# Expert blocks of 96 + 32 slots issued as four column strips of 32 slots on TensorE

## The chip, the cores and the metric

One core of one Trainium2 chip runs the whole program; nothing is shared with other cores. The metric is the device time of one execution in microseconds (us), as the median of several runs. In the profile PE is TensorE's matmul row, PEld its weight loads, DVE VectorE, ACT ScalarE, POOL GpSimd, SP SyncE.

## What is computed

One layer on 512 latent tokens (and 256 context tokens) of width 1024: an RWKV-7 head group and an HGRN2 head group behind one input projection, an output projection, and then a mixture of experts, where this change lies:

```python
def _swiglu(x, wg, wu, wd):
    return (jax.nn.silu(x @ wg) * (x @ wu)) @ wd

scores = jax.nn.sigmoid(h @ router_w)
...
_, top_e = lax.top_k(sel, TOP_K)              # 8 of 64 experts for each of the 512 tokens
gate = gate / jnp.sum(gate, axis=-1, keepdims=True) * ROUTE_SCALE
...
def step(out, inp):
    tok, gw, e = inp                          # a block of slots of one expert
    y = _swiglu(h[tok], wg[e], wu[e], wd[e]) * gw[:, None]
    return out.at[tok].add(y), None
```

Each expert has three float32 matrices: gate and up of 1024 x 256, down of 256 x 1024, 1 MB each, 3 MB in all. Every expert's weights are read from memory once.

## The kernel before

The first 1090 us of the program (mixers, output projection, router, shared expert) are not touched. What follows is the routed experts, until about 1942 us, and a final norm.

**Blocks.** Experts are ranked by size. A block has 128 slots (tokens) on 128 rows of the result. Of the 46 blocks 25 have one expert on all 128 slots, 11 have two experts with 64 slots each, and 10 (`NMIX`) have a larger expert on slots 0 to 95 and one of the smallest on slots 96 to 127. The last two kinds need the weights of two experts: 6 MB. The three are called whole, 64 + 64 and 96 + 32 here. A list written at line 1650 mixes the kinds in proportion.

**One block.** `front` (line 1726) makes `xT`, the block's tokens transposed: for 30 blocks an indirect DMA on POOL's queue gathers the rows (line 1740) and TensorE transposes them (line 1746); for 16 blocks TensorE picks them from rows on chip with 96 small matmuls (line 1735). `ffn_in` (line 1462) multiplies: for each of 8 tiles of 128 channels, `xT` is the stationary operand and the weights, gate beside up, 512 columns, are the moving one (line 1467). `ffn_out` (line 1470) applies silu on ACT (line 1472) and the product on DVE (`av`, line 1474), transposes on TensorE (line 1478), copies on ACT (`at`, line 1480), and multiplies with the down weights, 2 halves of 512 columns by 2 tiles (line 1485). `add_rows` (line 1681) scales the result on DVE (`rows`, line 1686) and adds it to the sums in memory with an indirect DMA of 512 KB on POOL's queue (line 1687).

A block's experts are given as `halves`, a list of (slots, activations, weights). Each half is one matmul instruction per tile, which writes the rows of its slots in one PSUM bank:

```python
for kt in range(8):
    for r, lhs, w in halves:
        pe.matmul(pg[r], lhs(kt), w[0][:, :, kt * 256:kt * 256 + 256], start=(kt == 0), stop=(kt == 7))
```

A column strip is the part of TensorE's array whose columns write certain rows of the result: a half on slots 64 to 127 occupies the columns 64 to 127. Instructions on different columns can run at the same time.

**Order.** TensorE works in program order: `xT` and line 1467 of a block, then lines 1478 and 1485 of the block before it. A scheduler lays out the instructions of each engine; the small matmuls of line 1735 and the lists (line 1628: which tokens a later block takes) fill places between.

**Weights.** SP's queue issues one DMA of 1 MB each for gate, up and down of one expert after another (`load`, line 1371, the DMA at line 1378). A load waits for two things: that the load two places before it has landed (`LAG` = 2 in flight), and that its buffer is free. There are five buffers for experts (`NWL` + `NWR`), so a load waits for the matmuls of the expert five places before it.

**Lists and sums.** The list of a block (`li`, line 1634, DVE) has four buffers, and the scatter of line 1687 reads it. So the list of block i + 4 waits until the scatter of block i has landed, and DVE, which works in order, has the products `av` and the `rows` of later blocks behind it. The gather and the scatter stand in one queue on POOL.

Of the kernel before, what the change touches and what calls it, by code (L numbers as in the profile page):

```python
# [8 lines left out]
F32 = mybir.dt.float32  # L9
FR = mybir.dt.float32r  # L10
# [13 lines left out]
NWL, NWR = 4, 1               # buffers for the weights of experts  # L24
LAG = 2                      # loads in flight
ONPE = range(12, 44, 2)      # blocks whose rows TensorE picks, from rows on chip; the others' come by DMA
HB = 4                       # block from which on these rows are loaded
NP = 4                       # experts whose weights come before the routing is known: they rank last
# experts by size: NONE have a block of 128 slots each, NMIX 96 slots of a block, NTWO are two to a block, and the
# smallest NMIX have the other 32 slots of the former  # L30
NONE, NMIX = 18, 10
NTWO = 64 - NP - NONE - 2 * NMIX
# pairs in the output projection, in the order in which they are ready
OUT = [[('rw', 0), ('hg', 0)], [('rw', 1), ('rw', 2)], [('hg', 1), ('hg', 2)], [('hg', 3), ('rw', 3)]]
# priorities of the streams along their steps, and the number of steps; smaller ones go first
# [11 lines left out]
def hybrid_layer(ctx, tc, x, c, xctx, c_ctx, w_mod, b_mod, norm1_g, norm2_g, w_in, rw_conv, rw_w0, rw_w2,  # L47
# [29 lines left out]
    # ---------------------------------------------------------------- constants  # L77
# [24 lines left out]
    # masks of the chunk scores, rows (B s | K s) for d 0 and (K s | B s) for d 1, columns (A t | R t)  # L102
# [11 lines left out]
    # scan resets  # L114
# [6 lines left out]
    # masks of the 32-token blocks of HGRN2, for two heads  # L121
# [15 lines left out]
    hTh = hp.tile([128, 8, NT], FR)             # hT = hTh + hTl, each exact in float32r  # L137
# [14 lines left out]
    # conditioning vectors, then per-channel vectors, rows of 128 turned into columns  # L152
# [13 lines left out]
    lo = const.tile([128, 2, 8], F32)          # lb, 1 - lb  # L166
# [9 lines left out]
    def vectors():  # L176
# [20 lines left out]
        # lower bounds of HGRN2: softmax over the two rows, first entry  # L197
        l3 = vc[:, VR['hlb']:VR['hlb'] + 16].rearrange("p (d l j) -> p d l j", d=2, l=2)
        lv = lbt.rearrange("p (d j) k -> p d j k", d=2)
        # softmax with its maximum: k 0 max, 1 e0, 2 e1, 3 sum  # L200
# [10 lines left out]
    # adaLN: silu of the conditioning vectors as a stationary operand  # L211
# [24 lines left out]
    # operands of a step of the scan, both directions: (K' B')^T d, (A | R) d, scores d h, inverses h  # L236
    WCT = {False: 64, True: 128}
    PKW = {lat: 256 + 6 * w + 128 for lat, w in WCT.items()}
    # operands of HGRN2: queries and gates, values with tokens on partitions, forget gates
# [9 lines left out]
    H2_d = dt("h2", (NACC, D))                  # rows that unused slots take are zero  # L249
    ACC = dt("acc", (2 * NACC, D))              # sums of the routed experts, the first and the second of a block  # L250
    X_d = dt("xl", (128, 512))                  # of the blocks beyond the slots: per token, slot and gate
# [3 lines left out]
    # until the scans begin, the place of the mixers' results serves the convolutions  # L255
    cv_a = pers.tile([128, 2048], F32, tag="y_rw")
    cv_b = pers.tile([128, 2048], F32, tag="y_hg")
    PC = const.tile([128, 4, 2, NCH], F32)      # decay of a chunk: pair, direction, step
    # ------------------------------------------------------------------ streams of work
    # The mixers run as streams that take turns, in steps; what a step needs of other streams is in marks.  # L260
# [6 lines left out]
    def banks(names):  # L267
        """PSUM in turns"""
        names = list(names)

        def get(name):
            names.append(names.pop(0))
            return psb(names[-1], name)
        return get

    # ---------------------------------------------------------------- projection
    # tiles of 128 columns: decay, rate, gate of RWKV-7; for pairs of heads its r, k, v or HGRN2's q, g, i, f
    porder = [(0, 'rw'), (1, 'rw'), (0, 'hg'), (2, 'rw'), (1, 'hg'), (3, 'rw'), (2, 'hg'), (3, 'hg')]
    NP1 = 6                  # of these before the scans begin
# [6 lines left out]
    def s_weights():  # L286
        """weights of the tiles, as the sum of two float32r parts"""
# [16 lines left out]
    # ------------------------------------------------- norm 1, adaLN, transposes  # L304
# [81 lines left out]
    def tok_major(src, dst, alloc):  # L386
        """dst [128, 6, 128] <- src [128, NT] transposed, tokens on partitions"""
        for g0, g1 in ((0, 4), (4, 6)):
            pt = alloc("p_tok")
            for g in range(g0, g1):  # L390
                pe.transpose(pt[:, (g - g0) * 128:(g - g0) * 128 + 128], src[:, g * 128:g * 128 + 128], ident)
            yield
            act.activation(dst[:, g0:g1].rearrange("p g v -> p (g v)"), pt[:, 0:(g1 - g0) * 128], AF.Copy)
            yield

    # ------------------------------- RWKV-7: operands of the scan, scores and inverses of the chunks
# [3 lines left out]
    y_0 = cpa.tile([128, SEQ], F32)              # result of the pair of heads that is scanned first  # L400
# [21 lines left out]
    def conv(n, m, pl, pcx, dst, out_):  # L422
        """dst [128, NT] (or lat only) <- depthwise conv of projection tile m"""
# [39 lines left out]
    def turned(src, dst):  # L463
        """tokens on partitions, to memory"""
# [5 lines left out]
    def s_evac():  # L470
        """what becomes of the projection's tiles"""
# [70 lines left out]
    def rw_head(j):  # L542
# [4 lines left out]
        # 1 / norm per head and token, with the tokens on partitions, spread over the channels again  # L547
# [29 lines left out]
    def rw_gates(j, d):  # L577
        """decay and rate of a direction, and what follows from them"""
# [23 lines left out]
        o = 1 - d                      # P_t at columns o .. o+63, 1 at the other end  # L602
        pool.memset(px[:, :, 64 * d:64 * d + 1], 1.0)
        act.activation(px[:, :, o:o + 64], cs.rearrange("p (c t) -> p c t", t=64), AF.Exp, scale=-KAPPA)
        act.activation(cs, cs, AF.Exp, scale=KAPPA)          # 1 / P
# [4 lines left out]
        # of the bonus, r times k over both directions  # L610
# [10 lines left out]
    def rw_oper(j, d):  # L621
        """operands of the scores in a direction"""
# [5 lines left out]
        # chunks in the order of the steps; tokens of A and B reversed within a chunk for d 1  # L628
# [31 lines left out]
    def pk(j, lat, f0, f1, rows=slice(0, 128)):  # L660
        """columns f0 .. f1 of the operands of the steps of pair j, as [rows, steps, columns]"""
# [10 lines left out]
    def rw_scores(j, d):  # L672
        """scores of the chunks in one direction, and the operands of the scan to memory"""
# [3 lines left out]
        for n in range(0, NCH, 2):  # L677
# [4 lines left out]
            st = xq.tile([128, 2, 2, 2, 64], F32, name="SC", bufs=2)             # step, A | R, h, t  # L682
# [19 lines left out]
        # the operands that the scan takes, K and B decayed to the end of the chunk  # L702
# [17 lines left out]
    def rw_bonus(j):  # L720
        """sum over the head of r * (kd_f + kd_b) * r_k, times v"""
# [12 lines left out]
    def s_scores():  # L734
        for j in range(4):
            if j > 1:
                yield from need(('merged', j - 2))
            st_[j]["SA"] = xq.tile([128, NCH, 2, 64], F32, name="SA", bufs=2)     # triangular parts, columns B s, A t
# [6 lines left out]
    def rw_inverse(j):  # L745
        """unit triangular systems: the inverses of the 32 x 32 blocks (d, q, n, h) on the diagonal, one to a partition"""
# [25 lines left out]
        # inverses of the 64 x 64 systems from those of the blocks on the diagonal: B^-1 = D + D U D  # L772
# [44 lines left out]
    def head_norm(sq, bank, eps):  # L817
        """1 / sqrt(mean + eps) per head and token of squares sq, over the head's channels in bank; tokens lie on
        partitions in between"""
# [29 lines left out]
    # ------------------------------------------------------------------- scan of RWKV-7 over the chunks  # L849
# [94 lines left out]
    def rw_out(j, pl, psn):  # L944
        """group norm, bonus, gate"""
# [30 lines left out]
    def inverse_tiles():  # L976
        """likewise, in the place of the inverses'"""
# [24 lines left out]
    def y_of(kind, j):  # L1002
        """result of a pair of heads, and its rows of the output projection"""
        return (y_0 if j == 0 else y_rw[:, j]) if kind == 'rw' else y_hg[:, j], j if kind == 'rw' else 4 + j

    # ------------------------------------------------------------------ HGRN2
    def hgrn_pair(j, hq, psg):
# [8 lines left out]
        for d in range(2):  # L1016
# [41 lines left out]
            # products of the decays of a group's four 32-blocks, in processing order  # L1058
# [14 lines left out]
            # level 1: later 32-block of a 64 against the earlier; level 2: later 64 against the earlier  # L1073
            qe4 = qe.rearrange("p (g n) b -> p g n b", n=4)
            ke4 = ke.rearrange("p (g n) b -> p g n b", n=4)
            qsec, ksec = (2, 0) if d == 0 else (0, 2)      # first block of the later and of the earlier 64
            odd = 1 - d                                    # parity of the later block of a 64
# [11 lines left out]
            # states at the borders of groups  # L1089
# [10 lines left out]
            # scores  # L1100
# [75 lines left out]
    # ------------------------------------ rest of adaLN, and HGRN2's part of the output projection  # L1176
    def s_mod(psm):
        """remaining adaLN rows, without their bias: g1, sh2, sc2, g2"""
# [45 lines left out]
    def out_rows(w, kind, j):  # L1224
        """rows of the output projection"""
# [4 lines left out]
    def s_out(pl, psm):  # L1230
        """the residual with the output projection of pairs as they are ready"""
# [3 lines left out]
        # sums that the routed experts add to, and rows for unused slots  # L1235
# [15 lines left out]
        for group in OUT:  # L1251
            ws = []
            for kind, j in group:
                # the last weights come early, to where the first pairs of HGRN2 were
# [23 lines left out]
    def run(done, waiting=""):  # L1278
        """the streams in turns, until those in done have ended and those in waiting wait for a mark"""
# [61 lines left out]
    # ===================================== output projection, norm 2, router, shared expert  # L1341
    psc[0] = ctx.enter_context(tc.tile_pool(name="psC", bufs=1, space=PSUM, reuse_waits="tile"))
    late = ctx.enter_context(tc.tile_pool(name="late", bufs=1, reuse_waits="tile"))
    # blocks of slots: the first NONE experts, second blocks of the largest five, pairs, 96 and 32 slots, the last NP
# [557 lines left out]
```

## Time and profile before

| | before |
|---|---|
| median of 3 runs | 1969.67 us (1947.13 to 1979.79) |
| span of the profiled execution | 1964.3 us (5.4 us under the median; it has no other time of its own) |
| TensorE busy | 1777.6 us, 90% |
| DVE, ACT, POOL busy | 753.9, 618.5, 395.2 us |
| moved by DMA | 401.65 MB, mean 204 GB/s |
| routed experts, 1095 to 1930 us of the span | 835 us |

A matmul's end in the trace is modelled: instructions follow each other 0.43 us apart where each is shown as 0.592 us long. So the time of a group is read from its first start to its last end in the timeline, and not from the mean of one. A float32 matmul of the program stands as two matmuls and two weight loads in the trace. A busy share is an average over a stretch.

### The profile page before, as it was taken

What the parts mean: (1) busy time and instruction counts of PE and PEld (TensorE: products, weight loads), DVE (VectorE), ACT (ScalarE), POOL (GpSimd) and SP (SyncE); (2) the same over time, 40 slices, a digit from 0 to 9 for tenths busy, and PEclk for the clock granted to TensorE, in tenths of its full rate; (3) what the DMA queues carried; (4) which work ended last, traced back from release to release, by engine and by line L of the source; (5) the groups of instructions that cost most, each with busy time, mean ns of one, the idle gap of its engine ahead of it and who ended that gap; (6) DMA issues with size and microseconds to landing.
All of it is one profiled execution on the core that took longest, in us unless ns stands there. A gap on an engine that the chain in (4) does not pass through costs nothing. (4 is left out here: it accounts for less than half of the span.)

```text
span 1964.3 us, 25497 instructions
## 1 busy us (share of the span) xinstructions
PE 1777.6 (90%) x9675; PEld 1004.8 (51%) x9675; DVE 753.9 (38%) x1722; ACT 618.5 (31%) x1286; POOL 395.2 (20%) x372
## 2 busy tenths in 40 slices
PE   5998989999699999898999889988899999799983
PEld 2766676675577775564455443333344443433431
DVE  4566685847563344433446332111121121111113
ACT  5463535345143353421323232111121221111121
POOL 2233223313221242231230012100111110101111
PEclk9977988998579977687999989999899999899987
DMA  7313555554565354533437877995967999758975
GB/s 257 94 50 108 148 137 147 174 137 134 129 210 144 114 185 139 169 128 124 141 124 281 296 259 245 333 348 204 318 204 249 311 324 335 247 187 296 350 238 161
DMA packets 200252, 401.65 MB, mean 204 GB/s; under 512 B 41804, under 2 KB 132009, under 8 KB 175168
## 3 DMA queue, kind: packets, MB, share of 16 engines
q1 hardware_dynamic: 188768, 360.05, 53.0%
q0 software_dynamic: 11360, 39.96, 9.1%
q8 instruction: 77, 1.26, 0.3%
q14 instruction: 47, 0.39, 0.1%
HBM read 323.66 MB, written 73.15 MB: 202 GB/s over the span
## 5 line engine op out<-in xcount | busy, mean ns | idle before, releaser
L1467 PE MATMUL p_gu<-wgu,xT 128*64 128x512 f32 (+3 forms) x1104 | 424.1, 605 | 0.4 <-ACT xT L1458 0.4
L1467 PEld LDWEIGHTS p_gu<-wgu,xT 128*64 128x64 f32 (+3 forms) x1104 | 129.1, 155 | 254.0 <-issue 240.2
L1485 PE MATMUL p_y<-wd,at 128*64 128x512 f32 (+3 forms) x584 | 240.8, 636 | 4.4 <-ACT at L1480 3.0
L369 PE MATMUL p_proj<-hTh,w_hi 128*128 128x512 f32 (+1 forms) x456 | 181.5, 398 | 6.0 <-ACT w_hi L296 3.1
L370 PE MATMUL p_proj<-hTh,w_lo 128*128 128x512 f32 (+1 forms) x456 | 176.3, 388 | 3.8 <-DVE w_lo L298 3.8
L371 PE MATMUL p_proj<-hTl,w_hi 128*128 128x512 f32 (+1 forms) x456 | 177.3, 390 | 2.3 <-POOL hTl L351 1.7
L1687 POOL DMA_INDIRECT acc<-rows,li x46 | 74.3, 1616 | 463.6 <-DVE rows L1686 443.4
L1634 DVE SCALAR_TENSOR_TENSOR li<-lv,bpr 128x2 int32<-128x2 f32 x46 | 10.1, 219 | 401.1 <-DMA acc<-rows,li 287.9
L1485 PEld LDWEIGHTS p_y<-wd,at 128*64 128x64 f32 (+3 forms) x584 | 71.2, 162 | 141.8 <-issue 124.0
L1472 ACT ACTIVATE sl<-p_gu 128x256 f32<-128x256 f32 x50 | 19.2, 384 | 384.9 <-PE p_gu L1467 383.4
L1458 ACT ACTIVATE xT<-p_xg,sh2c,s2c 128x128 f32<-128x128 f32 x240 | 90.1, 461 | 110.0 <-PE p_xg L1746 109.7
L1686 DVE SCALAR_TENSOR_TENSOR rows<-p_y,lv,g2r 128x512 f32<-128x512 f32 x92 | 68.2, 746 | 147.3 <-PE p_y L1485 147.1
L369 PEld LDWEIGHTS p_proj<-hTh,w_hi 128*128 128x128 f32 x456 | 94.7, 208 | 28.4 <-issue 6.1
L371 PEld LDWEIGHTS p_proj<-hTl,w_hi 128*128 128x128 f32 x456 | 94.4, 207 | 21.7 <-issue 5.6
L370 PEld LDWEIGHTS p_proj<-hTh,w_lo 128*128 128x128 f32 x456 | 94.6, 208 | 19.6 <-issue 4.6
L1740 POOL DMA_INDIRECT xg<-h,li x30 | 31.4, 1047 | 346.6 <-issue 158.1
L1735 PE MATMUL p_xs<-sel,h2p 128*128 128x128 bf16 x1536 | 92.9, 219 | 0.0
L1735 PEld LDWEIGHTS <-h2p 128*128 128x128 bf16 x1536 | 87.4, 98 | 9.5 <-issue 9.2
L687 PE MATMUL p_sc<-AR,BK 64*128 64x128 f32 (+1 forms) x384 | 64.9, 341 | 20.0 <-DVE SC L689 9.1
L1458 ACT ACTIVATE xT<-p_xs,sh2c,s2c 128x128 f32<-128x128 f32 x128 | 48.2, 458 | 105.5 <-PE p_xs L1735 105.5
L1474 DVE TENSOR_TENSOR av<-sl,p_gu 128x256 f32<-128x256 f32 x50 | 30.1, 602 | 115.8 <-ACT sl L1472 115.8
L687 PEld LDWEIGHTS p_sc<-AR,BK 64*128 64x128 f32 x384 | 50.5, 228 | 41.3 <-issue 12.8
(520 smaller groups left out, 2716.8 us busy)
## 6 DMA issues: line engine op xcount, KB each, us to landing
wgu<-in_exp_w_gate_dram SPq DMA_DIRECT2D x64, 1024.0 KB, 6.7
wgu<-in_exp_w_up_dram SPq DMA_DIRECT2D x64, 1024.0 KB, 8.4
wd<-in_exp_w_down_dram SPq DMA_DIRECT2D x64, 1024.0 KB, 6.3
w_raw<-in_w_in_dram SPq DMA_DIRECT2D x35, 512.0 KB, 4.1
wm<-in_w_mod_dram SPq DMA_DIRECT2D x32, 512.0 KB, 3.8
pkt<-pk SPq DMA_DIRECT2D x24, 576.0 KB, 4.7
wm<-in_w_mod_dram SPq DMA_DIRECT2D x8, 1024.0 KB, 8.3
pk<-SC SPq DMA_DIRECT2D x32, 256.0 KB, 3.5
```

Source lines behind the costliest of these rows:

```text
L369: pe.matmul(o[k], wh[:, kt, :], hTh[:, kt, s], start=(kt == 0), stop=False)
L370: pe.matmul(o[k], wl[:, kt, :], hTh[:, kt, s], start=False, stop=False)
L371: pe.matmul(o[k], wh[:, kt, :], hTl[:, kt, s], start=False, stop=(kt == 7))
L687: pe.matmul(p3[:, i], bk[r, n + i, :], ar[r, n + i, 0:w], start=True, stop=True)
L1458: act.activation(dst[:, kt, :], v, AF.Identity, scale=s2c[:, kt:kt + 1], bias=sh2c[:, kt:kt + 1])
L1467: pe.matmul(pg[r], lhs(kt), w[0][:, :, kt * 256:kt * 256 + 256], start=(kt == 0), stop=(kt == 7))
L1474: dve.tensor_tensor(av.rearrange("s t p -> s p t"), sl.rearrange("s (p t) -> s p t", t=2), pg[:, 256:512].rearrange("s (p t) -> s p t", t= ...
L1485: pe.matmul(py[n][r], at[:, t * 128 + r.start:t * 128 + r.stop], w[1][:, t * 1024 + n * 512:t * 1024 + n * 512 + 512], start=(t == 0), sto ...
L1686: dve.scalar_tensor_tensor(yo[:, cs_], py[n], g, g2r[:, cs_], op0=OP.mult, op1=OP.mult)
L1687: pool.indirect_dma_start(out=ACC if two else ACC[0:NACC], in_=yo, in_offset=None, compute_op=OP.add, out_offset=bass.IndirectOffsetOnAxis ...
L1735: pe.matmul(pt[:, q * 128:q * 128 + 128], h2p[:, i, t, kt * 128:kt * 128 + 128], sel[:, t], start=(i == 0 and t == 0), stop=(i == 2 and t ...
L1740: pool.indirect_dma_start(out=xg.bitcast(F32), out_offset=None, in_=H2_d, in_offset=bass.IndirectOffsetOnAxis(ap=tok, axis=0))
```

## The change

A helper `strips` cuts the halves of a block into strips of equal width: 64 or 128 where the larger half has that many slots, otherwise 32. Whole blocks and 64 + 64 blocks come out as they were. A 96 + 32 block gives four strips of 32 slots, three with the larger expert's weights and one with the smaller's, each an instruction of its own at lines 1467 and 1485 (1473 and 1492 in the changed file). The rest of the diff takes out comments, and later lines stand 6 or 7 places lower.

```diff
+    def strips(halves):
+
+        n = max(r.stop - r.start for r, _, _ in halves)
+        n = n if n in (64, 128) else 32
+        return [(slice(a, a + n), a - r.start, lhs, w) for r, lhs, w in halves for a in range(r.start, r.stop, n)]
+
     def ffn_in(halves, pl):
...
-            for r, lhs, w in halves:
-                pe.matmul(pg[r], lhs(kt), w[0][:, :, kt * 256:kt * 256 + 256], start=(kt == 0), stop=(kt == 7))
+            for r, o, lhs, w in strips(halves):
+                pe.matmul(pg[r], lhs(kt)[:, o:o + r.stop - r.start], w[0][:, :, kt * 256:kt * 256 + 256],
+                          start=(kt == 0), stop=(kt == 7))
...
-                for r, lhs, w in halves:
+                for r, _, _, w in strips(halves):
```

The order on TensorE at the first 96 + 32 block and the block behind it, before (`p_gu` is the result of line 1467, `p_y` of line 1485, `p_bank` the transposes of line 1478, `p_xg` those of line 1746):

```order
L1467 MATMUL p_gu<-wgu,xT 96x512
L1467 MATMUL p_gu<-wgu,xT 32x512
L1467 MATMUL p_gu<-wgu,xT 96x512
L1467 MATMUL p_gu<-wgu,xT 32x512
L1478 MATMUL p_bank<-ident,av 128x128 x2
L1746 MATMUL p_xg<-identr,xg 128x128 x6
L1485 MATMUL p_y_8944<-wd,at 64x512 x4
L1485 MATMUL p_y_8945<-wd,at 64x512 x4
```

The same place in the changed kernel:

```order
L1473 MATMUL p_gu<-wgu,xT 32x512 x32
L1485 MATMUL p_bank<-ident,av 128x128 x2
L1753 MATMUL p_xg<-identr,xg 128x128 x6
L1492 MATMUL p_y_8960<-wd,at 64x512 x4
L1492 MATMUL p_y_8961<-wd,at 64x512 x4
```

The 16 alternating instructions of the first product (the last four of them stand above) became 32 of one shape; nothing beside them moved.

Where a 96 + 32 block comes behind a block whose rows TensorE picks, the scheduler puts the first tile's matmul ahead of the rest. Before, at the second such block:

```order
L1746 MATMUL p_xg<-identr,xg 128x128 x2
L1467 MATMUL p_gu<-wgu,xT 96x512
L1735 LDWEIGHTS h2p
L1735 MATMUL p_xs<-sel,h2p 128x128
L1735 LDWEIGHTS h2p
L1735 MATMUL p_xs<-sel,h2p 128x128
```

The same place in the changed kernel:

```order
L1753 MATMUL p_xg<-identr,xg 128x128 x2
L1473 MATMUL p_gu<-wgu,xT 32x512 x3
L1742 LDWEIGHTS h2p
L1742 MATMUL p_xs<-sel,h2p 128x128
L1742 LDWEIGHTS h2p
L1742 MATMUL p_xs<-sel,h2p 128x128
```

The larger expert's three strips of the first tile go ahead together where its one instruction went, and the other 29 follow where the other 15 stood. On SP and POOL no instruction changes its place, and on DVE and ACT a few change by one or some places.

## Rows read from the trace of the kernel before

**Rows 1.** Stretches of the routed experts: busy us by engine, granted clock, DMA share, GB/s.
```profile
1095.00:1930.00 835.00, 777.58 (x3790) 325.12 (x3789) 157.44 (x415) 175.04 (x466) 100.58 (x73) 0.96 0.82 278
1200.00:1300.00 100.00, 97.79 (x396) 34.44 (x396) 16.91 (x46) 20.47 (x56) 12.07 (x9) 0.98 0.92 319
1600.00:1700.00 100.00, 87.80 (x475) 37.83 (x473) 16.79 (x44) 19.53 (x54) 9.23 (x7) 0.95 0.86 296
1800.00:1900.00 100.00, 94.75 (x477) 38.23 (x476) 17.13 (x42) 22.00 (x60) 13.64 (x10) 0.99 0.94 320
1285.00:1300.00 15.00, 15.00 (x39) 4.66 (x38) 1.81 (x4) 2.98 (x9) 0.00 (x0) 1.00 1.00 404
...
1722.00:1748.00 26.00, 25.96 (x89) 7.45 (x86) 4.67 (x10) 4.34 (x12) 2.76 (x2) 1.00 0.42 122
```

**Rows 2.** What SP's queue waited for, 1095 to 1930 us: us, times, longest.
```profile
SPq L1378 <- DMA wgu<-in_exp_w_gate_dram: 213.3, 59, 6.2
SPq L1378 <- DMA wd<-in_exp_w_down_dram: 157.2, 53, 6.3
SPq L1378 <- DMA wgu<-in_exp_w_up_dram: 112.1, 46, 4.6
SPq L1378 <- PE p_y L1485: 93.2, 13, 20.7
SPq L1378 <- PE p_gu L1467: 32.3, 7, 11.8
...
SPq L1378 <- PE p_bank L1628: 24.3, 4, 11.8
SPq L1378 <- PE p_xg L1746: 11.6, 1, 11.6
```

**Rows 3.** TensorE's timeline: start us, us, operation; products of three kinds of blocks.
```profile
1500.15 16.08 PE L1467 MATMUL p_gu<-wgu,xT 128*96 128x512 f32 x32
...
1517.07 3.65 PE L1485 MATMUL p_y<-wd,at 128*64 128x512 f32 x16
...
1526.03 7.08 PE L1467 MATMUL p_gu<-wgu,xT 128*128 128x512 f32 x16
...
1533.86 8.09 PE L1485 MATMUL p_y<-wd,at 128*96 128x512 f32 x16
...
1542.27 7.09 PE L1467 MATMUL p_gu<-wgu,xT 128*64 128x512 f32 x32
...
1550.20 3.70 PE L1485 MATMUL p_y<-wd,at 128*128 128x512 f32 x8
```

**Rows 4.** Timeline: a product on four strips of 32 columns (line 332).
```profile
36.09 1.94 PE L332 MATMUL p_mod<-wm,sil 128*32 128x512 f32 x16
```

**Rows 5.** Timeline: strips of 32 columns one after another (line 1203).
```profile
715.94 4.24 PE L1203 MATMUL p_mod<-wm,sil 128*32 128x512 f32 x9 [0.30 <-DMA wm<-in_w_mod_dram]
```

**Rows 6.** TensorE's groups, 1095 to 1930 us: busy us, mean ns, idle before, releaser.
```profile
L1746 PE MATMUL p_xg<-identr,xg 128*128 128x128 f32 x232 | 32.9, 268 | 12.7 <-DMA xg<-h,li 12.7
L1478 PE MATMUL p_bank<-ident,av 128*128 128x128 f32 x92 | 20.4, 304 | 34.8 <-DVE av L1474 32.0 <-DVE lv L1631 1.9 <-DVE lv L1632 0.9
```

**Rows 7.** POOL's timeline around one long wait: scatter, gather, scatter.
```profile
1656.40 1.61 POOL L1687 DMA_INDIRECT acc<-rows,li  x1 [28.56 <-DVE rows L1686]
1669.32 1.01 POOL L1740 DMA_INDIRECT xg<-h,li  x1 [11.30 <-issue]
1670.63 1.58 POOL L1687 DMA_INDIRECT acc<-rows,li  x1 [0.30 <-issue]
```

**Rows 8.** DVE's timeline at the end of that wait.
```profile
1684.25 0.22 DVE L1634 SCALAR_TENSOR_TENSOR li<-lv,bpr 128x2 int32<-128x2 f32 x1 [14.41 <-DMA acc<-rows,li]
1684.39 0.59 DVE L1474 TENSOR_TENSOR av<-sl,p_gu 128x256 f32<-128x256 f32 x1
```

**Rows 9.** TensorE's timeline at the end of that wait.
```profile
1685.03 0.69 PE L1478 MATMUL p_bank<-ident,av 128*128 128x128 f32 x2 [11.51 <-DVE av L1474]
```

**Rows 10.** DMA issues, 1095 to 1930 us: KB each, median us to landing.
```profile
acc<-rows,li POOLq DMA_INDIRECT x45, 11.3
```

## The prediction

> **What bounds the kernel now.** I read the stretches of the expert phase first, then the waits of the queue of loads, then the timelines of single blocks. The phase from 1095 to 1930 us lasts 835 us. TensorE is busy in 777.6 us of it and the DMA engines for a share of 0.82, that is 835 x 0.82 = 685 us of full transfers [rows 1]. So TensorE bounds the phase on the average, and DMA stands 12% behind it. The average hides that they take turns. In the waits of SP's queue the loads stand for 482.6 us behind loads that have not landed (the three rows with a DMA as releaser), where DMA is the limit. They stand for 161.4 us behind TensorE's matmuls, which still hold a buffer (the four rows with PE) [rows 2]. The stretch from 1722 to 1748 us shows the second case: TensorE busy all the time, DMA at 0.42 [rows 1]. A 96 + 32 block's product lies in it.
>
> TensorE's 57 idle us in the phase come from elsewhere: 32.0 us before the transposes of line 1478, which wait for DVE's `av`, and 12.7 us for gathered rows [rows 6]. In the longest of these waits DVE did not work either. It stood 14.41 us at the list of a later block, until a scatter had landed, and `av` came behind that list [rows 8, 9]. From one scatter to the next there it took 1670.63 - 1656.40 = 14.2 us [rows 7]. This chain (scatter lands, list, gather issued, next scatter) repeats once a block, so 46 blocks would need 46 x 14.2 = 655 us if all went at that pace. It is a third limit, close to the other two.
>
> **What the change takes from TensorE.** A 96 + 32 block spends 16.08 us in the first product and 8.09 us in the second, 24.17 us together. A 64 + 64 block does the same arithmetic, also with two sets of weights, in 7.09 + 3.65 = 10.74 us, as long as a whole block (7.08 + 3.70 us) [rows 3]. Its two halves run side by side on different columns, while the 96 and the 32 run one after the other.
>
> Do four strips run side by side as well? One product early in the program answers that. 16 matmuls of 32 columns took 1.94 us on four strips of one PSUM bank [rows 4], while 16 matmuls of a whole block took 7.08 us [rows 3]. 1.94 us is four times the 0.44 us of one such matmul (7.08 / 16) and 0.2 us for the end, so all four strips worked at once. In the changed kernel the first product of a 96 + 32 block has 8 tiles of 4 strips, 64 matmuls in the trace: 16 turns of 0.44 us, 7.09 us like the 64 + 64 block. The second has 4 x 4 rows, 32 matmuls, 8 turns, 3.65 us. That is 24.17 - 10.74 = 13.43 us per block, and 134 us for the 10 blocks. Nothing is added on another engine and no DMA is added or moved. The weight loads of the strips (three times as many for the larger expert) lie under the matmuls of other strips, as they do in rows 4; without that cover each turn would be longer by the 0.11 to 0.17 us that the shown loads of strips take, at most 24 x 0.17 = 4 us a block, 41 us in all. Where the scheduler puts the first tile ahead of the rest, 3 strips go ahead instead of one instruction of 96; that costs one turn pair either way, and I take nothing for it.
>
> The Trainium skill has measured packing as less than perfect: "TensorE: Matmul & The Clock Gate", Part 3, under the measured speedup against the span model, gives 3.07 times for four row tiles of 512 columns, not 4. An estimate by that figure: the products would take 10.74 x 4 / 3.07 = 14.0 us a block, and the change would take 102 us from TensorE instead of 134. The row of this kernel shows no such loss beyond the 0.2 us at the end, and the measured row decides.
>
> **What of it reaches the end.** After the change TensorE needs 777.6 - 134 = 643 us, DMA still 685 us, the scatter chain up to 655 us. DMA becomes the limit, and the other two are within 6% of it, so they cannot hide under it: each has stretches of its own where it is the late one. A phase of exactly 835 - 134 = 701 us would ask of DMA a share of 685 / 701 = 0.98 throughout. Over 100 us the shares are 0.86 to 0.94 in the three stretches shown [rows 1]. I take 0.92, that of the stretch from 1200 to 1300 us, as the one in which loads went nearly without a break while blocks of all kinds passed: 685 / 0.92 = 745 us, a gain of 90 us. The share of 0.94 gives 729 us, a gain of 106; the share of 0.86, in the stretch that holds the wait of rows 7 to 9, gives 797 us, a gain of 38. The upper bound is TensorE's 134 us. A gain below zero is excluded by these limits as long as strips overlap, since none of the three grows.
>
> What is late next: the 161 us in which loads waited for TensorE shrink to a third or less, and TensorE in turn waits for weights, which it hardly does now, and for more scatters, since a scatter that shares the DMA engines with loads lands after 11.3 us by the median [rows 10]. TensorE's idle gaps lower its clock: in the whole phase the granted clock is 0.96, in the stretch with the 11.51 us wait 0.95 [rows 1, 9]. With as much idle time everywhere that is 1% of 643 us, 6 us; the DMA-bound sum covers it.
>
> The sum: 1964.3 - 90 = 1874 us for the profiled execution. The median of the runs is 5.4 us above that execution, so 1879.7, rounded to 1879 us.
>
> **Rivals.**
> - *The scatter chain or bursts decide.* Loads stay as unsteady as in the stretch at 0.86: gain 38 us, 1964.3 + 5.4 - 38 = 1932 us. For it: the 14.2 us from scatter to scatter [rows 7], longer than the 11.5 us or so that a changed two-expert block needs on TensorE. Against it: all waits for `av` in the phase are 32.0 us [rows 6], and that one alone is 11.51 of them [rows 9].
> - *All of it arrives.* DMA reaches 0.98, gain 134 us, 1836 us. For it: DMA did stand at a share of 1.00 with 404 GB/s from 1285 to 1300 us [rows 1]. Against it: that stretch is 15 us long, and this needs the whole phase to be better than its best 100 us.
> - *Two strips at a time.* The two matmuls that the trace shows for each float32 instruction are on the same strip. If TensorE begins matmuls strictly in program order, the second of them blocks the next strip until the first has ended, and only the second of one strip and the first of the next overlap: 32 turns of 0.44 us, 14.1 us, and 16 turns, 7.1 us, for the second product. The gain is 24.17 - 21.2 = 3 us a block, 30 us in all, TensorE stays the bound, and the time is 1940 us. Against it: rows 4, where a whole set of 16 would have taken 3.5 us, not 1.94. The Trainium skill has this rule ("TensorE: Matmul & The Clock Gate", Part 3, the mechanism): matmuls start and end in strict program order. The trace does not agree with it for strips, by the 1.94 us.
> - *Strips one after another: slower.* Place: lines 1467 and 1485 of the 10 blocks. In rows 4 every strip had moving data of its own; here three strips stream the same weights from the same addresses, which no row shows. If those three took turns instead, and the fourth with them, 32 instructions of 7.08 / 8 = 0.885 us would take 28.3 us and 16 of 3.70 / 4 = 0.925 us 14.8 us, 43.1 in place of 24.17, 189 us in all: 2159 us. Strips do run one at a time in another place (9 in 4.24 us) [rows 5], there because each waits for its own load. The point from which this is a loss: fewer than 43.1 / 24.17 = 1.8 strips at work on the average.
>
> **How the numbers follow.** My forecast (four strips, DMA at 0.88 to 0.95) has a chance of 0.62. The chain or bursts have 0.15, all of it 0.10, two strips 0.07, one strip at a time 0.06. The range of 8 in 10 runs from the full gain, 1836 us, to 1932 us at a share of 0.86. What is left out is the two cases of missing overlap and a part of the bursts. About 2%, 39 us, can be told from no change with this kernel. Faster by more than that: 0.62 + 0.10 and most of the bursts case, whose middle lies at that bound but whose upper half does not, 0.12, so 0.84. Within 2%: the rest of that case and two strips, 0.10. Slower: 0.06.
>
> **What would show it.** In the changed profile the product of a 96 + 32 block should stand as one row of x64 with 7.1 us, and its second product x32 with 3.7 us. If they read 14 and 7 us, the overlap is of two strips, and above 16 us my main step is wrong. SP's waits for TensorE should fall from 161 to some 60 us or less and those for landings stay near 480 us; the DMA share of the phase should be 0.90 to 0.94, TensorE's busy time in it some 645 us. The transposes of line 1478 should wait for `av` as long as now or longer. If instead the DMA share stays under 0.87 while TensorE idles for over 130 us, the scatter chain has taken the place of DMA.

## The result, and the profile after

| | before | changed |
|---|---|---|
| median of the runs | 1964.77 us (1947.13 to 1979.79) | 1886.53 us (1872.8 to 1894.35) |
| ratio, with its 95% interval | 1 | 0.9614 (0.9545 to 0.9683) |
| span of the profiled execution | 1964.3 us | 1871.0 us |
| first routed product to last | 838.4 us (1094.2 to 1932.6) | 743.3 us (1096.3 to 1839.6) |

The change makes the kernel faster by 78 us of the median, 62 to 89 us by the interval, against a forecast of 1879 us. A second measurement of the same kernel (below) gave a ratio of 0.953 (0.9474 to 0.9585). The last line of the table is used from here on as the *phase*. It leaves out the start of the routed experts, which moves between 1082 and 1109 us among the executions of this study, for reasons that lie ahead of the change. But a phase comes from one profiled execution: the changed kernel, measured twice, shows 743.3 and 753.0 us, and the same with six list buffers 728.6 and 715.4, so two executions of one kernel differ in it by 10 to 13 us. In the profiled pair the phase became 95 us shorter.

First the timeline of TensorE in the changed kernel, the answer to [rows 3]:

```profile
1475.15 7.07 PE L1473 MATMUL p_gu<-wgu,xT 128*32 128x512 f32 x64
...
1499.87 3.64 PE L1492 MATMUL p_y<-wd,at 128*32 128x512 f32 x32
...
1503.83 7.09 PE L1473 MATMUL p_gu<-wgu,xT 128*64 128x512 f32 x32
...
1520.64 1.06 PE L1473 MATMUL p_gu<-wgu,xT 128*32 128x512 f32 x6
...
1523.91 8.66 PE L1473 MATMUL p_gu<-wgu,xT 128*32 128x512 f32 x58 [2.21 <-DMA wgu<-in_exp_w_up_dram]
```

64 matmuls of 32 columns take 7.07 us, as long as the 64 + 64 block (the row of 7.09 us), and the second product takes 3.64 us. Before they took 16.08 and 8.09 us. So the four strips work at once, also where three of them stream the same weights. The last two rows show what the sum did not have. In six of the ten blocks the first tile's three strips go ahead by themselves (x6, 1.06 us) and the remaining 58 take as long as all 64 would, 7.05 us at the full clock. One of them, the last row, also waited 2.21 us for its weights, and then ran slowly: 8.66 us in place of 7.05.

The stretches, to be read beside [rows 1] (busy us by engine, granted clock, DMA share, GB/s):

```profile
1095.00:1836.00 741.00, 667.75 (x4279) 318.02 (x4277) 156.03 (x417) 176.21 (x469) 100.17 (x72) 0.95 0.92 313
1200.00:1300.00 100.00, 81.85 (x522) 36.90 (x519) 17.70 (x51) 22.13 (x61) 13.67 (x10) 0.91 0.94 318
...
1500.00:1600.00 100.00, 94.12 (x704) 43.95 (x704) 20.30 (x55) 22.72 (x63) 12.67 (x9) 0.95 0.98 340
1600.00:1700.00 100.00, 97.51 (x696) 48.00 (x689) 21.52 (x59) 24.12 (x67) 14.27 (x10) 1.00 0.99 337
```

The DMA share rose from 0.82 to 0.92 and the rate from 278 to 313 GB/s. TensorE's busy time fell from 777.6 to 667.75 us. It idles 73 us in the stretch, where it idled 57. The clock, 0.96 before, is 0.95.

What SP's queue of loads waited for, beside [rows 2] (us, times, longest), 1095 to 1836 us:

```profile
SPq L1378 <- DMA wgu<-in_exp_w_gate_dram: 208.4, 59, 6.6
SPq L1378 <- DMA wd<-in_exp_w_down_dram: 185.4, 56, 6.2
SPq L1378 <- DMA wgu<-in_exp_w_up_dram: 111.1, 51, 4.3
...
SPq L1378 <- PE p_bank L1635: 34.7, 6, 11.5
SPq L1378 <- PE p_xg L1753: 12.7, 4, 11.6
...
SPq L1378 <- PE p_gu L1473: 9.6, 4, 8.9
SPq L1378 <- PE p_bank L1485: 6.7, 3, 6.0
...
SPq L1378 <- PE p_y L1492: 4.1, 3, 3.3
```

The five waits for TensorE add up to 67.8 us. Before, the four rows shown in [rows 2] were 161.4 us, and the fifth, for `p_bank` of line 1478, another 6.3. The three for landings add up to 504.9, where they were 482.6. The loads now wait nearly always for loads.

TensorE's groups (busy us, mean ns, idle before and who ended it), with [rows 6] as their counterpart, and in a second fence three of the waits of all engines in the same stretch (us, times, longest):

```profile
L1473 PE MATMUL p_gu<-wgu,xT 128*64 128x512 f32 x416 | 104.9, 626 | 10.6 <-DMA wgu<-in_exp_w_up_dram 10.4 <-ACT xT L1458 0.3
...
L1473 PE MATMUL p_gu<-wgu,xT 128*32 128x512 f32 x640 | 82.2, 626 | 2.2 <-DMA wgu<-in_exp_w_up_dram 2.2
...
L1753 PE MATMUL p_xg<-identr,xg 128*128 128x128 f32 x240 | 34.2, 269 | 20.8 <-DMA xg<-h,li 20.8
L1485 PE MATMUL p_bank<-ident,av 128*128 128x128 f32 x92 | 20.2, 301 | 26.1 <-DVE av L1481 25.2 <-DVE lv L1639 0.9
```

```profile
DVE li L1641 <- DMA acc<-rows,li: 299.8, 30, 14.0
...
PE p_bank L1485 <- DVE av L1481: 25.2, 5, 8.4
...
PE p_gu L1473 <- DMA wgu<-in_exp_w_up_dram: 15.9, 6, 5.7
```

TensorE's idle time has three owners of about the same size: `av` 25.2 us, gathered rows 20.8, weights 15.9, the last of which was not there before. Behind `av` stands the list that waits for a scatter, 30 times and 299.8 us of DVE's time.

### The profile page after: what moved, and what is told of

Same layout as the page of the kernel before. It is cut to its first block, busy times and chain, and to the rows that moved or that the text cites. A ratio compares the mean times of both kernels' runs of the same rounds, so it can differ in the third digit from the quotient of the medians.

```text
span 1871.0 us, 26459 instructions
## 1 busy us (share of the span) xinstructions
PE 1667.0 (89%) x10155; PEld 994.6 (53%) x10155; DVE 751.0 (40%) x1722; ACT 618.0 (33%) x1286; POOL 397.2 (21%) x372
## 5 line engine op out<-in xcount | busy, mean ns | idle before, releaser
L1473 PE MATMUL p_gu<-wgu,xT 128*32 128x512 f32 (+2 forms) x1424 | 353.7, 621 | 16.6 <-DMA wgu<-in_exp_w_up_dram 15.9
L1473 PEld LDWEIGHTS p_gu<-wgu,xT 128*32 128x32 f32 (+2 forms) x1424 | 125.9, 143 | 202.4 <-issue 178.9
L1492 PE MATMUL p_y<-wd,at 128*32 128x512 f32 (+2 forms) x744 | 198.0, 621 | 4.8 <-ACT at L1487 3.6
L1641 DVE SCALAR_TENSOR_TENSOR li<-lv,bpr 128x2 int32<-128x2 f32 x46 | 10.1, 219 | 411.3 <-DMA acc<-rows,li 299.8
L1492 PEld LDWEIGHTS p_y<-wd,at 128*32 128x32 f32 (+2 forms) x744 | 66.3, 147 | 102.1 <-issue 89.2
L298 DVE TENSOR_TENSOR w_lo<-w_raw,w_hi 128x1024 fp32r<-128x1024 f32 x35 | 46.3, 1323 | 42.4 <-ACT w_hi L296 42.4
```

Of the source, the lines that this page charges most:

```text
L298: dve.tensor_tensor(wl, w, wh.bitcast(F32), OP.subtract)
L1473: pe.matmul(pg[r], lhs(kt)[:, o:o + r.stop - r.start], w[0][:, :, kt * 256:kt * 256 + 256], start=(kt == 0), stop=(kt == 7))
L1492: pe.matmul(py[n][r], at[:, t * 128 + r.start:t * 128 + r.stop], w[1][:, t * 1024 + n * 512:t * 1024 + n * 512 + 512], start=(t == 0), sto ...
```

## Experiments

Twelve measurements. Changes are against the changed kernel unless said otherwise. Where only one profiled execution is compared, that is said.

**The first product alone on strips** (line 1492 as before):

```diff
-                for r, _, _, w in strips(halves):
+                for r, _, w in halves:
```

> Strips at the first product alone (line 1467), the second as before. Theory (strips overlap, DMA then limits): TensorE loses 10 x 9.0 = 90 us and needs 688 us in the expert phase, as much as DMA's 685; gain against before 60 to 80 us, so nearly all that the whole change gives. Rival (TensorE is still the limit after the change): gain is 90/134 of the whole change's, about 52 us.

Measured: 1902.23 us, ratio 0.9692 (0.9616 to 0.9768), 64 us less than before. The phase is 783.5 us, 55 less than before.

**The second product alone on strips** (line 1473 as before):

```diff
-            for r, o, lhs, w in strips(halves):
-                pe.matmul(pg[r], lhs(kt)[:, o:o + r.stop - r.start], w[0][:, :, kt * 256:kt * 256 + 256],
-                          start=(kt == 0), stop=(kt == 7))
+            for r, lhs, w in halves:
+                pe.matmul(pg[r], lhs(kt), w[0][:, :, kt * 256:kt * 256 + 256], start=(kt == 0), stop=(kt == 7))
```

> Strips at the second product alone (line 1485). TensorE loses 10 x 4.45 = 44 us and stays the limit: both theories expect a gain against before of 35 to 44 us by the theory, 26 us by the rival with equal shares. If DMA limits after the whole change, the gains of the two parts add up to more (100 to 120 us) than the whole gives (78 us); if not, they add up to it.

Measured: 1932.53 us, ratio 0.9845 (0.976 to 0.993), 34 us less. The phase is 795.1 us, 43 less. By the phase the parts add up to the whole (55 + 43 = 98 beside 95 us), by the medians they are more than it (64 + 34 beside 78), with intervals some 15 us wide on each side. So neither shows a ceiling that the full change runs into and its parts don't, and with this noise neither excludes one. The two theories written down for the first part are not told apart: its 64 us lie in the range of the one (60 to 80), its 55 us of the phase near the 52 of the other. Of the 90 us that the first product takes from TensorE 55 arrive in the phase of that execution, of the second's 44 nearly all.

**Strips of unequal width**: 64 and 32 slots of the larger expert and 32 of the smaller, three instructions in place of four.

```diff
     def strips(halves):
+        if any(r.stop - r.start == 96 for r, _, _ in halves):
+            (r, lhs, w), (r2, lhs2, w2) = halves
+            return [(slice(0, 64), 0, lhs, w), (slice(64, 96), 64, lhs, w), (slice(96, 128), 0, lhs2, w2)]
```

> The larger expert's 96 slots as strips of 64 and 32, the smaller's as 32: three instructions instead of four. Theory A (strips overlap when they have the same width): per tile two turns for the 64 and two for the two strips of 32, the first product takes 14 to 16 us, ratio to before 0.99 to 1.00. Theory B (it is enough that columns are apart): all three overlap, first product 7.1 us, ratio 0.96 as with four strips.

Measured: 1966.07 us, ratio 1.0008 (0.9971 to 1.0045): all of the gain is gone. The timeline of this kernel says why:

```profile
1501.46 15.95 PE L1476 MATMUL p_gu<-wgu,xT 128*64 128x512 f32 x48
```

15.95 us are 2.0 us a tile, or four turns of 0.50 us. The starts of one tile's matmuls in the trace (us, columns):

```
1501.459 64
1501.940 64
1502.462 32
1502.469 32
1502.916 32
1502.922 32
1503.445 64
```

The two strips of 32 start 7 ns apart, on different columns. The strip of 64 runs beside neither. The Trainium skill has a rule for it in "TensorEngine Tiling (Array Packing)", Key Properties: a change of the tiling mode, as distinct from a change of tile, drains TensorE. The trace agrees. A turn across a change of width takes 0.52 us, one within a width 0.45 to 0.48. So the equal width of `strips` is what the gain rests on here, and not the cutting as such.

**Six list buffers** (`lv` and `li`), so that the list of block i + 6 waits for the scatter of block i:

```diff
-        lv = late.tile([128, 8], F32, name="lv", bufs=4)
+        lv = late.tile([128, 8], F32, name="lv", bufs=6)
...
-        li = late.tile([128, 2], I32, name="li", bufs=4)
+        li = late.tile([128, 2], I32, name="li", bufs=6)
```

> The changed kernel with six buffers for the lists instead of four, so that a list no longer waits for the scatter four blocks before. Theory (DMA limits): DVE's waits for scatters go, TensorE's 25 us of waits for av go in part, but the loads come no faster: 0 to 12 us less than the changed kernel. Rival (the chain from scatter to scatter took DMA's place): 30 us or more less than the changed kernel, ratio to before under 0.945.

Measured: 1852.56 us, ratio 0.9427 (0.9372 to 0.9482), 34 us below the changed kernel of the first measurement. That is what the rival expected, and more than the 12 us that DMA as the limit allowed. DVE's waits for the scatter are gone, and with them TensorE's for `av`. TensorE's waits in this kernel (us, times, longest):

```profile
PE p_gu L1473 <- DMA wgu<-in_exp_w_up_dram: 37.8, 11, 6.7
PE p_xg L1753 <- DMA xg<-h,li: 11.1, 2, 10.7
...
PE p_bank L1485 <- DVE av L1481: 2.3, 4, 1.2
```

25.2 us of waiting for `av` became 2.3, and 15.9 us of waiting for weights became 37.8. That fits an engine that came earlier to the next product and found its weights not landed. Its idle time in the phase fell from 73 to 64 us.

**Two thirds of the weights.** To take load off the DMA engines alone, the up weights are not loaded and the gate weights serve for both; the up projection is left out by that. The edit in the kernel before (first) and in the changed one (the same, with the strips):

```diff
-        for dst, src in ((wgu[:, 0], exp_w_gate), (wgu[:, 1], exp_w_up), (wd, exp_w_down)):
+        for dst, src in ((wgu[:, 0], exp_w_gate), (wd, exp_w_down)):
...
-                pe.matmul(pg[r], lhs(kt), w[0][:, :, kt * 256:kt * 256 + 256], start=(kt == 0), stop=(kt == 7))
+                pe.matmul(pg[r], lhs(kt), bc(w[0][:, 0:1, kt * 256:kt * 256 + 256], [128, 2, 256]), start=(kt == 0), stop=(kt == 7))
```

> The kernel before without the DMA of the up weights (the gate weights serve for both, so the up projection is left out as such; TensorE's work is the same). 60 MB of 189 MB fewer, DMA's work falls from 685 to some 500 us. Theory (before, TensorE limits): 0 to 25 us less than before. Rival (DMA limited already): over 60 us less.

> The changed kernel without the DMA of the up weights, as in the run beside it. Theory (after the change DMA limits): TensorE's 643 us and some 50 us of waits remain, so 30 to 55 us less than the changed kernel, and the gap to the kernel before with the same loads is 110 to 134 us, near the whole 134 us that TensorE was spared. Rival (something else limits after the change): 0 to 15 us less than the changed kernel, the gap stays near 80 us.

Measured: 1893.43 us, ratio 0.963 (0.9575 to 0.9685), and 1770.12 us, ratio 0.8994 (0.8951 to 0.9037). In size both missed my theory. The kernel before, which I took for bound by TensorE, gives 72 us back when its loads are lighter, as the rival had it. The changed kernel gives 107 to 116 us, where 30 to 55 were expected. The gap between the two is 123 us, as expected, and the phases stand 769.7 and 644.2 us, 125.5 apart. The stretch of each:

```profile
1094.00:1860.00 766.00, 756.42 (x3789) 318.97 (x3788) 157.48 (x416) 173.51 (x461) 101.55 (x72) 1.00 0.69 221
```

```profile
1094.00:1745.00 651.00, 634.01 (x4294) 309.40 (x4294) 156.33 (x430) 176.21 (x470) 102.71 (x73) 0.99 0.82 261
```

TensorE idles 10 and 17 us, and its clock is 1.00 and 0.99. With light loads TensorE bounds both kernels and what the change takes from it arrives. TensorE's waits for `av` are gone in both as well, though the lists still have four buffers and DVE still waits for scatters, here in the kernel before:

```profile
DVE li L1634 <- DMA acc<-rows,li: 272.4, 27, 12.5
```

So the chain from scatter to scatter held up TensorE beside the full loads, and not beside two thirds of them.

**Three loads in flight** in place of two, with all weights:

```diff
-LAG = 2
+LAG = 3
```

> The changed kernel with three loads in flight instead of two. Theory (DMA engines limit, share 0.92 in the phase and 0.97 to 0.99 from 1500 us on): 0 to 15 us less than the changed kernel. Rival (the limit is the number of loads in flight, not the engines): 25 us or more less. If scatters suffer from the third load: up to 20 us more.

Measured: 1854.15 us, ratio 0.9445 (0.9397 to 0.9493), 23 to 32 us below the two measurements of the changed kernel. In the one profiled execution only 6 us of it lie in the phase (737.6 us), which is less than two executions of one kernel differ by; it began 14 us earlier. The stretch, and TensorE's waits there:

```profile
1081.80:1819.40 737.60, 659.48 (x4276) 315.73 (x4276) 154.41 (x417) 176.04 (x468) 102.18 (x73) 0.95 0.89 316
```

```profile
PE p_bank L1485 <- DVE av L1481: 44.9, 7, 10.9
PE p_xg L1753 <- DMA xg<-h,li: 22.7, 8, 7.2
```

Waits for weights are down from 15.9 to 0.4 us, and the waits for `av` are up from 25.2 to 44.9. This is the picture of the six list buffers, turned round: each cause, removed, leaves time to the other. TensorE idles 78 us of the phase, no less than the 73 of the changed kernel.

**The changed kernel again, and six list buffers in both kernels.** Three kernels beside each other, to see whether the scatter chain falls on the changed kernel more than on the one before.

> The changed kernel once more, beside the three others on one chip: ratio to before 0.955 to 0.968, as measured first. It is the measure for the three beside it.

> The changed kernel with six list buffers, again, beside the changed kernel. If the chain from scatter to scatter has a part in what limits the changed kernel: 10 to 35 us less than it, ratio to before 0.940 to 0.955. If the first measurement was chance: within 8 us of it.

> The kernel before with six list buffers. TensorE waited 32 us for av in its profile, all behind such lists. Theory (the chain costs both kernels alike, and DMA alone took back 40 to 56 us of the 134): 25 to 35 us less than before, ratio 0.982 to 0.988, and the gap between the kernels with six buffers stays near 78 us. Rival (the chain took back a part of the gain, as blocks got shorter than its 14 us): 0 to 12 us less than before, and the gap with six buffers grows to 100 us or more.

Measured: 1877.18 us, 0.953 (0.9474 to 0.9585); 1854.49, 0.9429 (0.9373 to 0.9486); 1930.58, 0.9851 (0.98 to 0.9902), beside a kernel before of 1963.62. The buffers give the changed kernel 23 us (34 by the first measurement) and the kernel before 33. So the chain is no price of the change: it stood in both, and the gap between the two with six buffers is 76 us, no larger than without (86 in the same measurement).

**Both at once, in the changed kernel and in the one before.** Six list buffers and three loads in flight, the two edits shown above.

> The changed kernel with six list buffers and three loads in flight. If the two wait for different things, their gains add: 1820 to 1840 us, ratio 0.925 to 0.938. If DMA's engines are the common limit: no better than either alone, ratio 0.940 to 0.946.

> The kernel before with six list buffers and three loads in flight, the fourth corner beside the changed kernel with both (1794 us). Theory (with a good feed TensorE is the limit of both kernels, so the strips' gain rises from 78 towards 123 us, the gap measured with a third of the loads left out): TensorE's work of some 756 us at full clock bounds it, 1885 to 1905 us, ratio 0.960 to 0.970, gap 90 to 110 us. Rival (the feed helps both kernels alike, the gap stays 78 us): 1872 us or less, ratio 0.953 or less.

Measured: 1794.31 us, ratio 0.9147 (0.9104 to 0.9191), and 1931.51 us, ratio 0.9806 (0.9756 to 0.9856). In the changed kernel the two edits together take 83 us off the 1877.18 measured beside them, against 23 and 23 for each alone; counted from the first measurement, 1886.53, it is 92 against 34 and 32. Either way together they give more than the sum, and more than either theory had (1820 to 1840 us at best). In the kernel before, the third load in flight adds nothing that stands clear of the intervals to the list buffers (ratio 0.9851, 1930.58 us), which neither theory had. The phases are 667.6 and 793.8 us, 126 apart. The medians lie 137 apart, but were measured beside different runs of the kernel before (1963.62 and 1970.58); by the ratios it is 130. In the profiled pair another 25 us had come about before the first routed product. The stretches, first the changed kernel:

```profile
1083.00:1750.60 667.60, 643.43 (x4276) 307.05 (x4276) 160.08 (x417) 174.18 (x468) 102.23 (x73) 0.99 0.96 349
1400.00:1500.00 100.00, 99.77 (x790) 48.61 (x787) 24.37 (x62) 25.84 (x71) 15.72 (x11) 1.00 1.02 388
```

```profile
1107.70:1901.50 793.80, 769.26 (x3796) 322.19 (x3796) 160.17 (x417) 174.22 (x468) 102.78 (x73) 0.99 0.82 293
```

TensorE works 643.43 of 667.6 us in the one and 769.26 of 793.8 in the other, idle for 24 us in each. Both stand at TensorE's own limit, and there the change is worth what it takes from TensorE. And the waits of TensorE in the changed kernel with both:

```profile
PE p_xg L1753 <- DMA xg<-h,li: 12.6, 3, 9.1
...
PE p_bank L1485 <- DVE av L1481: 2.3, 4, 1.2
PE p_gu L1473 <- DMA wgu<-in_exp_w_up_dram: 1.5, 1, 1.5
```

This kernel is the fastest of those that compute the whole program, 8.5% below the kernel before and 4 to 5% below the changed one.

## Why the prediction was right, and where it was not

*What the change takes from TensorE* (forecast 134 us). The two products came out at 7.07 and 3.64 us for 7.09 and 3.65. The term for the first tile, taken as nothing, was wrong: three strips that go ahead take two turns by themselves, and the fourth takes two more with the rest, 1.06 + 7.05 us in place of 7.07. Before, the split block cost 1.07 + 15.08, for 16.08 in one piece. With six such blocks that is 6 us, so 128 are left. TensorE's busy time at nearly full clock, 769.26 - 643.43 = 126 us, agrees within 2 us. The weight loads of the strips stayed hidden, as taken. Of the rivals, two strips at a time and one after another are excluded by the 7.07 us. In the block at 1475.15 us the first matmuls of the four strips start within 0.02 us of each other, and their second ones 0.45 us later. Whether that breaks program order, as the prediction says, depends on the order in which these matmuls are issued, which no run here shows; what failed is the rival's picture of one strip's second matmul blocking the next strip. The Trainium skill's 3.07 times for four tiles ("TensorE: Matmul & The Clock Gate", Part 3, measured speedup) is given for row tiles. The estimate from it, 14.0 us a block, is not borne out for these column strips: 7.07 + 3.64 is 10.71 us.

*What of it reaches the end* (forecast 90 us of the phase). The share of 0.92 was met to the digit, and 95 us arrived. What is missing from 126 can be read from the stretches. Over the two phases TensorE was busy 781.0 and 670.2 us. Against the pair at a clock of 0.99 (769.26 and 643.43) that is 12 us more before and 27 us more after, which took 15 us of the gain. Most of it is the clock: by the traces' records TensorE was busy at the lower level, 0.50, for 35.5 us before and 58.0 us after. At half the rate that costs 18 and 29 us, 11 more after the change. The other 4 us stay open. Its idle time rose from 57 to 73 us, which took 16 more: 126 - 15 - 16 = 95. The prediction put 6 us on the clock, about half of those 11. That its phase of 745 us came so near to 743.3 is in part luck: with 645 us of TensorE's work it held 100 us of idle time, and the trace has 670 us of work and 73 idle. By the medians less arrived, 78 us, because the changed kernel's median stands 15.5 us above its profiled span (1886.53 and 1871.0), where the prediction took 5.4 over from the kernel before.

*DMA as the limit, at 685 us.* Here the step failed, though its number fitted. It took 835 x 0.82 as an amount of DMA work that must be done, so that a phase of 701 us would ask for a share of 0.98 throughout. With six list buffers and three loads in flight the same loads passed in a phase of 667.6 us at a share of 0.96, which is 641 us, and at 388 GB/s over 100 us; the changed kernel shows 337 to 340 GB/s at 0.98 and 0.99. So a share does not stand for a fixed amount moved. Share times length is 685 and 682 us in the kernel before and the changed one, and 680 to 685 us with six list buffers alone, but 656 us with the third load alone, and 641 and 651 us with both edits. So the 685 us belong to two loads in flight. The DMA engines were not the limit there. The number of loads alone was not either, since the third load without the list buffers left the phase at 737.6 us; the limit was the two kinds of waiting together.

*The scatter chain cannot hide.* It was put as a third limit within 6% of the others, each late in stretches of its own. For the chain and the loads that was right, and is what the experiments show: list buffers alone move the wait to weights (37.8 us), a third load alone moves it to `av` (44.9 us), and only both leave TensorE 24 idle us. The wait of [rows 7 to 9] was not the longest, as the prediction has it: that one lasted 12.23 us, at 1330 us, and had the same shape, with DVE 15.32 us at a list until a scatter had landed. As a rival that *takes the place* of DMA it was wrong, since it stood in both kernels (33 and 23 us). That the transposes would wait for `av` "as long now or longer" was wrong as well: 25.2 us for 32.0, while the waits for weights and gathered rows grew (15.9 from nothing, and 20.8 from 12.7). An engine that has already waited for the one comes later to the other; that is a reading, and the exchange in the two kernels with one cause removed fits it.

*TensorE bounds the phase on the average.* Before, TensorE was busy 93% of the phase, and still two thirds of the weights gave 72 us. Over the phase its idle time fell from 57 to 10 us and its busy time from 781.0 to 760.1, at a clock of 1.00 for 0.96. So the average had hidden a price that loads took from TensorE in the kernel before as well, in idle time and in clock. The prediction saw the idle time, but counted the busy time as work.

*SP's waits* went to 67.8 us (forecast some 60 or less) and 504.9 (about 480): right in kind, a little short in size. The 161.4 us that it starts from leave out a fifth row of 6.3 us.

Open: how much of the third load alone is real in the phase, 6 us in one execution or the 23 to 32 of the medians, and by what a transfer occupies its engine longer with two loads in flight than with three. And the start of the routed experts, 1082 to 1109 us, was not looked into.

## What to carry to other kernels

Where instructions use only part of TensorE's columns, cut them all to the same width, so that they run beside each other; the cut into unequal widths gained nothing here. When an engine is relieved, look for every chain that is close to it and remove them together: one at a time they hand the wait to each other, and 23 and 23 us became 83. A DMA share near 1 is no proof that DMA is at its limit; try one more load in flight before believing it.

## What the runs showed of the hardware that was not expected

- Column strips overlapped with strips of their own width, and not with others, in the widths tried: 64 matmuls of 32 columns in 7.07 us, 48 of widths 64, 32 and 32 in 15.95 us.
- A DMA share of 0.99 went with 337 GB/s over 100 us with two loads in flight, and a share of 1.02 with 388 GB/s over 100 us with three. Two in flight can also reach more for a short time: 404 GB/s at 1.00 over 15 us in the kernel before, with POOL idle [rows 1].
- The granted clock fell behind short idle times, and the product after them paid. The stretches around one wait of the changed kernel, and that product in the timeline:

```profile
1380.00:1390.00 10.00, 5.89 (x20) 1.68 (x22) 2.06 (x5) 2.13 (x6) 1.18 (x1) 0.66 0.99 363
1391.50:1395.50 4.00, 1.01 (x11) 0.95 (x10) 1.22 (x4) 0.00 (x0) 1.58 (x1) 0.82 0.85 251
1395.90:1399.30 3.40, 3.40 (x17) 0.78 (x20) 0.00 (x0) 0.00 (x0) 0.00 (x0) 0.50 0.84 214
1395.89:1405.42 9.53, 9.53 (x59) 2.25 (x58) 0.22 (x1) 0.00 (x0) 0.00 (x0) 0.74 0.88 303
```

```profile
1394.73 1.23 PE L1753 MATMUL p_xg<-identr,xg 128*128 128x128 f32 x8 [2.99 <-DMA xg<-h,li]
1395.89 9.53 PE L1473 MATMUL p_gu<-wgu,xT 128*32 128x512 f32 x58
```

  TensorE was busy 5.89 us of 10 and 1.01 of 4. The product behind that began at a granted clock of 0.50, the lower level of 1.2 GHz, had 0.74 over its whole length, and took 9.53 us in place of 7.05 (9.53 x 0.74 = 7.05): 2.5 us on top of the 7 idle us of these two stretches. Over the phase the clock was 0.96 and 0.95 where TensorE idled 57 and 73 us, and 0.99 where it idled 24.
